# One hybrid decoder layer on one core: the gate weights' low parts on VectorE, and some work put behind the second norm's second root

## The chip, the cores and the metric

The kernel runs on one core of a Trainium2 chip. It uses TensorE (PE in the profile), VectorE (DVE), ScalarE (ACT), GpSimd (POOL) and SyncE (SP), which here only issues transfers. The metric is the device time of one execution in microseconds (us); less is better. Every quoted time of the kernel before is from its runs or its one profiled execution.

## The reference

One layer of a hybrid decoder for 1024 prompt positions and 8 x 8 sample positions, width 1024, hidden width 2816, all in float32:

```python
h = rms_norm(x, norm_mix_g)
proj = h @ w_in
...                                   # convolution heads a, attention heads o
x = x + jnp.concatenate([a, o], axis=-1) @ w_out
h = rms_norm(x, norm_ffn_g)           # the second norm
g_full = jnp.concatenate([ffn_past, h @ w_ffn_gate], axis=1)
g = depthwise_conv_valid(g_full, ffn_conv_w, ffn_conv_b)
x = x + (jax.nn.silu(g) * (h @ w_ffn_up)) @ w_ffn_down
```

The change lies between the last part of `@ w_out` and the first products with `w_ffn_gate` and `w_ffn_up`.

## The kernel before

**Numbers.** Each float32 operand of a product is split in a high part (ScalarE rounds it with a copy) and a low part (the operand less its high part, on VectorE or GpSimd); three matmuls stand for one: high by high, low by high, high by low. Tiles have 128 partitions. Activations lie transposed, as 8 tiles `x2` of 128 x 1088 (1024 prompt and 64 sample positions), worked on in two halves of 544 columns (HN).

**Order.** Tiles of a pool are handed out by tag; a tile laid where an older one was waits for the older one's last users. A scheduler then puts every engine's instructions in one order, which the engine follows strictly; `tc.issue_after(y)` keeps an instruction behind y in that order. Line numbers below are those of the kernel before; in the changed kernel they are 1 to 3 higher behind the edits.

**The stretch around the change** (some 557 to 690 us of the profiled execution):

1. `load_input` loads the mixer's last two tiles by halves (`mx`, high `mh` at line 991, low `ml` at 992). The last slices of `w_out` come as `wr`; `parts_of` (lines 976 to 980) makes their high part on ScalarE (978) and low part on GpSimd (979). Last of all it does the same for the four half tiles of the first gate weights (`gate_raw`; parts `wa`, `wb`).
2. `out_half(0)`: for each of 8 tiles m, matmuls (`g`), then VectorE adds them to `x2` (line 1148), ScalarE squares (1153, `sq`), VectorE sums the squares (1157). Then `out_half(1)` for the second half of the columns; its first three tiles have a deferred part of the product besides.
3. **First root**: `root` adds the squares over partitions with ten matmuls by a column of ones (line 209), and VectorE and ScalarE take the reciprocal root (213 to 224; the square root itself is 219). In PE's order these ten stand behind two tiles of `out_half(1)`. The low parts of the first up weights (1179, VectorE) stand behind the root. `spread` lays the root over partitions (transposes, line 236; copy `rb`, 238). VectorE then scales `x2` (1162), and `split` makes high (1051) and low parts (1052) of block b11 (tiles 0 to 3) and b21 (4 to 7).
4. `first_half(gate0)`: products of the first gate pair with b11 into two PSUM tiles `px`, `py`, copies of them (`ta`, 1200), products with b21, copies again (`c1`, 1205). The **second root** lies between these: its ten matmuls in the last step of b21, its transposes behind it.
5. `early_sums(w_gate, 1)` forms two sums of the second gate pair's weights on VectorE (1086 to 1088, tiles `s` and `wr`) and splits them (high 1075 on ScalarE, low 1076 on GpSimd).
6. `first_half(up0)`, and `second_half` for gate and up with blocks b22 and t1. From here on each pair is seven block products instead of eight, out of sums of blocks (Strassen-like), until 1080 us, when the down projection begins.

```python
        def early_sums(w, j):
            ...
            with tc.issue_after(made[7]):              # the low part of b21's last tile
                nc.vector.tensor_add(s1, u1, u2)
```

Of the kernel before, what the change touches and what calls it, by code (L numbers as in the profile page):

```python
# [18 lines left out]
F32 = mybir.dt.float32  # L19
F32R = mybir.dt.float32r  # L20
AF = mybir.ActivationFunctionType
# [3 lines left out]
P = 128  # L25
# [37 lines left out]
ORDER, DEFER = (4, 5, 6, 7, 0, 1, 2, 3), 3  # L63
# [20 lines left out]
def trunk_kernel(tc, xT, w_in, w_out, w_gate, w_up, w_down, par, kc, vc, sa, sf, pmask, smask,  # L84
                 yT, kT, vT, ca, cas, cf):
    nc = tc.nc
    with (
# [8 lines left out]
        def nm(s):  # L96
            cnt[0] += 1
            return f"{s}_{cnt[0]}"
# [23 lines left out]
        def zt(z, tag, bufs, s, w=N, dt=F32):  # L122
            return zone[z].tile([P, w], dt, tag=tag, name=nm(s), bufs=bufs)
# [76 lines left out]
        rooted, summed, copied, squared = [None], [None], [None], [None]  # L200
# [84 lines left out]
        wr = [wp.tile([P, D], F32, tag="WR", name=nm("wr"), bufs=WR) for _ in range(2)]  # L285
        w0 = [[wp.tile([P, D], F32R, tag="W", name=nm(s)) for s in ("wh", "wl")] for _ in range(2)]
        h = []
# [620 lines left out]
        def pair(s="g", tag="g2"):  # L908

            return zone[pairs[0] + "ps"].tile([P, 1024], F32, tag=tag, name=nm(s), bufs=pairs[1])  # L910
# [4 lines left out]
        def slot(tag, s, dt=F32R, w=HN):  # L915
            return zt("F", tag, 8, s, HN, dt)[:, :w]
# [17 lines left out]
        def two_products(outs, ws, x, start, hook=lambda k, last: None):  # L934


            n = HN // 2
            nk = len(x)
            last = None
            for k, (xh, xl) in enumerate(x):  # L940
                with tc.issue_after(last) if last else nullcontext():
                    for o, (whi, wlo) in zip(outs, ws):
                        for c in range(2):
                            ps = o[:, PO:512] if c == 0 else o[:, 512:PO + HN]
                            t = slice(c * n, c * n + n)
                            nc.tensor.matmul(ps, whi[:, k, :], xh[:, t], start=(start and k == 0), stop=False,
                                             skip_group_check=True)
                            nc.tensor.matmul(ps, whi[:, k, :], xl[:, t], start=False, stop=False,
                                             skip_group_check=True)
                            end = nc.tensor.matmul(ps, wlo[:, k, :], xh[:, t], start=False, stop=(k == nk - 1),  # L950
                                                   skip_group_check=True).ins
                last = end
                hook(k, last)

        def all_of(ps):
            return ps[:, PO:PO + HN]
# [15 lines left out]
        n1 = PARTS[-2]  # L972
# [3 lines left out]
        def parts_of(raw, hi, lo):  # L976

            done = nc.scalar.activation(hi, raw, AF.Copy).ins
            nc.gpsimd.tensor_sub(lo, raw, hi.bitcast(F32))
            return done  # L980
# [3 lines left out]
        def load_input(i, h, tag):  # L984
            nonlocal last_load, last_high
            raw = slot("b11", "mx", F32)
            with tc.issue_after(last_load):
                last_load = nc.sync.dma_start(raw, mixed[k0 + i][:, h * HN:h * HN + HN]).ins
            hi, lo = early[tag].pop() if early[tag] else slot(tag, "mh"), slot(tag, "ml")
            with tc.issue_after(last_high):  # L990
                last_high = nc.scalar.activation(hi, raw, AF.Copy).ins
            lows_made.append(nc.vector.tensor_sub(lo, raw, hi.bitcast(F32)).ins)
            part[h].append((hi, lo))
# [4 lines left out]
        def queued(dst, src):  # L998
            nonlocal last_load
            with tc.issue_after(last_load):  # L1000
                last_load = nc.sync.dma_start(dst, src).ins

        last_load, last_high = weights_read[0], turned_out[0]
        wl = [None] * KT
        raw_wd = {m: slot("b22", "wr", F32, n1 * P) for m in ORDER[:DEFER]}
        for h, tag in enumerate(("b11", "t2")):
            load_input(0, h, tag)
            for m0 in ORDER[h * 4:h * 4 + 4:2]:
                raw = slot("t1", "wr", F32, 2 * n * P)
                queued(raw.rearrange("p (m c) -> p m c", m=2), w_out[m0:m0 + 2, :, k0 * P:].rearrange("m p c -> p m c"))  # L1010
                if m0 == ORDER[h * 4]:
                    load_input(1, h, tag)
                hi, lo = early["b21"].pop() if early["b21"] else slot("b21", "wh", w=512), slot("b21", "wl", w=512)
                with tc.issue_after(last_high):
                    last_high = parts_of(raw, hi, lo)
                hi, lo = [t.rearrange("p (k c) -> p k c", c=P) for t in (hi, lo)]
                for j in range(2):
                    wl[m0 + j] = hi[:, j * n:j * n + n], lo[:, j * n:j * n + n]
# [6 lines left out]
        for i in range(n1):  # L1025
            hi, lo = slot("t3", "mh"), slot("t3", "ml")
            raw = lo.bitcast(F32)
            queued(raw, mixed[kd + i][:, HN:])
            with tc.issue_after(last_high):
                last_high = parts_of(raw, hi, lo)  # L1030
            highs.append(last_high)
            deferred.append((hi, lo))
        for m in ORDER[:DEFER]:
            hi, lo = [slot("b22", t, w=n1 * P) for t in ("wh", "wl")]
            with tc.issue_after(last_high):
                last_high = parts_of(raw_wd[m], hi, lo)
# [4 lines left out]
        gate0 = [[t.rearrange("p (k c) -> p k c", c=P) for t in x] for x in tiles]  # L1041
        for r, (hi, lo) in zip(gate_raw, tiles):
            with tc.issue_after(last_high):
                last_high = parts_of(r, hi, lo)

        blocks = {tag: [None] * 4 for tag in BTAGS}
        made, high = [], [None]
# [12 lines left out]
        def weight_raw(w, j):  # L1060
            raw = []
            for i in (j, j + HF):
                raw.append(wp.tile([P, D], F32, tag="WR", name=nm("wr"), bufs=WR))
                with tc.issue_after(last_load):
                    nc.sync.dma_start(raw[-1], w[i])
            return raw

        def block_tile(x, zone=False):

            if zone:  # L1070
                t = zt("F", "WA", 2, "wa", D, F32R)
            else:
                t = wp.tile([P, D], F32R, tag="W", name=nm("wb"))
            hi, lo = t[:, :half], t[:, half:]
            nc.scalar.activation(hi, x, AF.Copy)  # L1075
            nc.gpsimd.tensor_sub(lo, x, hi.bitcast(F32))  # L1076
            return [t.rearrange("p (k c) -> p k c", c=P) for t in (hi, lo)]

        def early_sums(w, j):

            g, u = weight_raw(w, j)
            g1, u1, u2 = g[:, :half], u[:, :half], u[:, half:]
            t = zt("F", "us", 1, "s1", 3 * HN)
            s1, s2 = t[:, :half], t[:, HN:HN + half]
            with tc.issue_after(made[7]):
                nc.vector.tensor_add(s1, u1, u2)
            nc.vector.tensor_sub(u1, g1, u1)
            nc.vector.tensor_sub(s2, s1, g1)
            with tc.issue_after(squared[0]):
                blocks = [block_tile(s2), block_tile(s1)]  # L1090
            return g, u, s2, blocks
# [101 lines left out]
        def first_half(w, between=lambda: None, hook=lambda k, last: None):  # L1193

            a11, a12, a21, a22 = w
            o = pair("px"), pair("py")
            two_products(o, (a11, a21), blocks["b11"], True)
            shared = [early["shared"].pop(0) if early["shared"] else zt("F", "tmp", 4, "ta", HN) for _ in o]
            for t, ps in zip(shared, o):
                nc.scalar.activation(t, all_of(ps), AF.Copy)  # L1200
            between()
            two_products(o, (a12, a22), blocks["b21"], False, hook)
            kept = [slot("t4", "c1", F32) for _ in o]
            for t, ps in zip(kept, o):
                nc.scalar.activation(t, all_of(ps), AF.Copy)
            return kept, shared

        def second_half(w):
# [6 lines left out]
        def between():  # L1215
            rs.append(root(sq1, D, HN))
# [6 lines left out]
        first_blocks(0, "b11")  # L1223
        first_blocks(4, "b21")
        g1, g_shared = first_half(gate0, between, spread_second)
        ready = early_sums(w_gate, 1)
        r1 = rs[1]
        for k in range(4):
            scale(1, k + 4, r1)
            split(x2[k + 4][:, HN:], "b22", k)  # L1230
        u1, u_shared = first_half(up0)
        for k, (x11, x12, x21, x22) in enumerate(quads):
            scale(1, k, r1)
# [386 lines left out]
        for i, (t0, n) in enumerate(TAIL):  # L1620
            r = []
# [111 lines left out]
```

## Time and profile before

| | |
|---|---|
| median of 3 runs | 1343.35 us (1338.85 to 1350.83) |
| profiled execution, its own time | 1340.95 us |
| its span in the profile | 1339.1 us (1.85 us lie around it) |
| busy: PE / DVE / ACT / POOL | 97% / 70% / 42% / 36% |
| granted PE clock, mean | 0.987 of full |

In rows of the timeline the columns are start, duration, engine, line, operation, output and inputs, shape, and how many are joined; brackets tell how long the engine had been idle and who released it. When several are joined, the duration is from the first one's start to the last one's end. In rows by stretch they are the stretch, its length, each engine's busy time with its instructions, the granted clock (1.00 is full), the share of the DMA engines, and GB/s. In rows of waits: the waiting group, who released it, total us, times, longest.

### The profile page before, as it was taken

The numbers are of one execution on the slowest core, as the hardware profiler recorded it, in microseconds if no ns is written. First come the engines' busy times: TensorE is split into PE (matmuls) and PEld (weight loads), VectorE is DVE, ScalarE is ACT, GpSimd is POOL, SyncE is SP. The second block draws the span as 40 slices with busy tenths as digits, with TensorE's granted clock in tenths as the row PEclk, the third lists the DMA queues.
The fourth block names the chain that finished last, engine by engine and source line by source line (L and its number), as shares of the span: only waits on it lengthen the run. The fifth ranks groups of instructions, "written<-read, shape, count | busy, mean of one in ns | idle before, by whom it ended". The sixth has DMA issues, their size and how long they took to land.

```text
span 1339.1 us, 25960 instructions
## 1 busy us (share of the span) xinstructions
PE 1298.5 (97%) x10302; PEld 1255.0 (94%) x10302; DVE 935.6 (70%) x1786; ACT 561.1 (42%) x1129; POOL 484.9 (36%) x393
## 2 busy tenths in 40 slices
PE   8999999999999998999999999999999989999996
PEld 7999998998988887899999999999999989999996
DVE  6379879565675666579986767667776569767656
ACT  6412121546675566345533323333333344334432
POOL 1312112111101101741665646556465434444610
PEclk9999999999999999989999999999999999999998
DMA  8248867565779867641113322133222395352403
GB/s 311 58 127 292 290 231 195 179 175 147 211 238 270 253 225 249 225 184 43 49 74 122 118 95 90 65 122 108 105 75 79 123 336 188 107 182 89 156 33 102
DMA packets 94233, 211.70 MB, mean 158 GB/s; under 512 B 13984, under 2 KB 43296, under 8 KB 94112
## 3 DMA queue, kind: packets, MB, share of 16 engines
q1 hardware_dynamic: 94112, 210.05, 47.7%
q8 instruction: 81, 1.33, 0.4%
q14 instruction: 40, 0.33, 0.1%
HBM read 153.97 MB, written 56.04 MB: 157 GB/s over the span
## 4 chain that ended last, share of the span: by engine, by line
PE 86%; DVE 7%; DMA 4%; ACT 2%; issue 1%; SPq 0%; DVEq 0%; ACTq 0%
PE g L187 6%; PE g L188 6%; PE g L189 6%; PE g L930 5%; PE g L929 5%; PE g L927 5%; PE py L929 4%; PE py L930 4%; PE py L927 4%; PE px L927 3%; PE px L930 3%; PE px L929 3%; PE pz L929 3%; PE pz L927 3%; PE pz L930 3%; PE o L747 3%
## 5 line engine op out<-in xcount | busy, mean ns | idle before, releaser
L163 POOL TENSOR_TENSOR wl<-wr,wh 128x1024 fp32r<-128x1024 f32 (+1 forms) x36 | 67.3, 1871 | 272.3 <-PE g L189 162.9
L187 PE MATMUL g<-xh,wh 128*128 128x384 f32 (+1 forms) x472 | 157.6, 334 | 2.1 <-DVE qkv L450 1.4
L188 PE MATMUL g<-xl,wh 128*128 128x384 f32 (+1 forms) x472 | 156.0, 330 | 0.0
L189 PE MATMUL g<-xh,wl 128*128 128x384 f32 (+1 forms) x472 | 155.8, 330 | 0.0
L929 PE MATMUL g<-ux,as 128*128 128x272 f32 x504 | 145.8, 289 | 3.6 <-DVE ux L1452 3.6
L930 PE MATMUL g<-ux,as 128*128 128x272 f32 x504 | 146.0, 290 | 0.0
L927 PE MATMUL g<-ux,as 128*128 128x272 f32 x504 | 145.6, 289 | 0.1
L1076 POOL TENSOR_TENSOR wb<-wr,wb 128x512 fp32r<-128x512 f32 x79 | 114.2, 1455 | 50.5 <-ACT wb L1075 50.5
L1467 POOL TENSOR_TENSOR as<-ar,as 128x640 fp32r<-128x640 f32 (+1 forms) x56 | 91.3, 1640 | 107.6 <-ACT as L1466 107.6
L1075 ACT ACTIVATE wb<-wr 128x512 fp32r<-128x512 f32 x79 | 49.6, 628 | 155.1 <-DVE wr L1110 95.1
L929 PEld LDWEIGHTS g<-ux,as 128*128 128x128 f32 x504 | 95.3, 189 | 4.3 <-DVE ux L1452 4.3
L1076 POOL TENSOR_TENSOR wa<-wr,wa 128x512 fp32r<-128x512 f32 x40 | 64.9, 1625 | 92.9 <-ACT wa L1075 75.6
L927 PEld LDWEIGHTS g<-ux,as 128*128 128x128 f32 x504 | 95.7, 190 | 0.3 <-ACT ux L1451 0.3
L930 PEld LDWEIGHTS g<-ux,as 128*128 128x128 f32 x504 | 95.5, 190 | 0.0
L187 PEld LDWEIGHTS g<-xh,wh 128*128 128x128 f32 x472 | 89.3, 189 | 4.7 <-issue 2.3
L1335 DVE SCALAR_TENSOR_TENSOR fc<-gb,prm,fc 128x1104 f32<-128x1104 f32 x44 | 81.6, 1875 | 14.8 <-ACT fc L1333 14.4
L699 ACT ACTIVATE y<-y,m 128x128 f32<-128x128 f32 (+1 forms) x192 | 88.5, 464 | 5.4 <-DVE m L687 5.0
L188 PEld LDWEIGHTS g<-xl,wh 128*128 128x128 f32 x472 | 89.4, 189 | 0.1
L189 PEld LDWEIGHTS g<-xh,wl 128*128 128x128 f32 x472 | 89.3, 189 | 0.1
L400 DVE SCALAR_TENSOR_TENSOR cacc<-gp,prm,cacc 128x1024 f32<-128x1024 f32 x60 | 84.6, 1410 | 0.1
L161 ACT ACTIVATE wh<-wr 128x1024 fp32r<-128x1024 f32 (+1 forms) x36 | 29.6, 821 | 130.4 <-PE g L189 92.5
L662 DVE CUSTOM_DVE_ANT_0 y<-s,pmk 128x128 f32<-128x128 f32 (+1 forms) x192 | 63.7, 377 | 27.3 <-PE s L658 22.1
(386 smaller groups left out, 4308.4 us busy)
## 6 DMA issues: line engine op xcount, KB each, us to landing
cr<-in_kc SPq DMA_DIRECT2D x24, 768.0 KB, 8.1
cr<-in_vc SPq DMA_DIRECT2D x24, 768.0 KB, 6.9
ux<-ub SPq DMA_DIRECT2D x63, 272.0 KB, 4.0
kk<-dk SPq DMA_DIRECT2D x48, 256.0 KB, 5.4
wr<-in_w_in SPq DMA_DIRECT2D x20, 512.0 KB, 4.8
wr<-in_w_gate SPq DMA_DIRECT2D x20, 512.0 KB, 3.3
wr<-in_w_up SPq DMA_DIRECT2D x20, 512.0 KB, 3.8
ub<-u SPq DMA_DIRECT2D x18, 544.0 KB, 4.3
```

The costliest lines, as they stand in the source:

```text
L163: lo_eng.tensor_sub(lo, raw, hi.bitcast(F32))
L187: nc.tensor.matmul(ps[c], whi[:, k, :], xh[:, t0:t0 + n], start=(k == 0), stop=False)
L188: nc.tensor.matmul(ps[c], whi[:, k, :], xl[:, t0:t0 + n], start=False, stop=False)
L189: nc.tensor.matmul(ps[c], wlo[:, k, :], xh[:, t0:t0 + n], start=False, stop=(k == nk - 1))
L400: eng.scalar_tensor_tensor(acc[:, :S], gp[:, j:j + S], col(w0 + j), acc[:, :S], op0=ALU.mult, op1=ALU.add)
L699: nc.scalar.activation(y, y, AF.Exp, bias=m[:, 4 * g + i:4 * g + i + 1], scale=-1.0, accum_out=den[:, g, 2 * hd + u, i:i + 1])
L927: nc.tensor.matmul(ps, whi[:, k, :], xh[:, t], start=(start and k == 0), stop=False, skip_group_check=True)
L929: nc.tensor.matmul(ps, whi[:, k, :], xl[:, t], start=False, stop=False, skip_group_check=True)
L930: last = nc.tensor.matmul(ps, wlo[:, k, :], xh[:, t], start=False, stop=(stop and k == nk - 1), skip_group_check=True).ins
L1076: nc.gpsimd.tensor_sub(lo, x, hi.bitcast(F32))
L1335: nc.vector.scalar_tensor_tensor(c[:, :W], gb[i][:, t:t + W], col(C_FW + 3 * f + t), c[:, :W], op0=ALU.mult, op1=ALU.add)
L1467: nc.gpsimd.tensor_sub(lo, raw, hi.bitcast(F32))
```

## The change

Three edits:

1. The low parts of the four gate half tiles are made on VectorE instead of GpSimd; the high parts stay on ScalarE.
2. `early_sums` of the second gate pair stands behind the end of the second root instead of behind b21's last low part; the `c1` copies of `px` and `py` stand behind the second root's square root.
3. Block b11's first tile `mx` is allotted ahead of block b22's three raw slices of `w_out`, so that the two tags change places in memory.

```diff
-        raw_wd = {m: slot("b22", "wr", F32, n1 * P) for m in ORDER[:DEFER]}
         for h, tag in enumerate(("b11", "t2")):
             load_input(0, h, tag)
+            if not h:
+                raw_wd = {m: slot("b22", "wr", F32, n1 * P) for m in ORDER[:DEFER]}
...
         for r, (hi, lo) in zip(gate_raw, tiles):
             with tc.issue_after(last_high):
-                last_high = parts_of(r, hi, lo)
+                last_high = nc.scalar.activation(hi, r, AF.Copy).ins
+            nc.vector.tensor_sub(lo, r, hi.bitcast(F32))
...
-            with tc.issue_after(made[7]):
+            with tc.issue_after(rooted[0]):
                 nc.vector.tensor_add(s1, u1, u2)
...
-            for t, ps in zip(kept, o):
-                nc.scalar.activation(t, all_of(ps), AF.Copy)
+            with tc.issue_after(squared[0]):
+                for t, ps in zip(kept, o):
+                    nc.scalar.activation(t, all_of(ps), AF.Copy)
```

**VectorE, end of `out_half(0)`.** `sq_6752` gathers the sum of squares, `x_1120` is the last tile of the first half, `x_1127` the first of the second half; `wa` and `wb` are the gate weights' parts. Before:

```order
L1148 TENSOR_TENSOR x_1120_6082<-g_6862,x_1120_6082 128x544
L1157 TENSOR_TENSOR sq_6752<-sq_6805,sq_6752 128x544
L1157 TENSOR_TENSOR sq_6752<-sq_6823,sq_6752 128x544
L1157 TENSOR_TENSOR sq_6752<-sq_6841,sq_6752 128x544
L1157 TENSOR_TENSOR sq_6752<-sq_6859,sq_6752 128x544
L1148 TENSOR_TENSOR x_1127_6122<-g_6880,x_1127_6122 128x544
L1157 TENSOR_TENSOR sq_6752<-sq_6877,sq_6752 128x544
L213 TENSOR_SCALAR rv_6940<-g_1295_6934 128x4
```

Now:

```order
L1150 TENSOR_TENSOR x_1120_6082<-g_6862,x_1120_6082 128x544
L1159 TENSOR_TENSOR sq_6752<-sq_6805,sq_6752 128x544
L1159 TENSOR_TENSOR sq_6752<-sq_6823,sq_6752 128x544
L1159 TENSOR_TENSOR sq_6752<-sq_6841,sq_6752 128x544
L1046 TENSOR_TENSOR wa_6611<-wr_6674,wa_6611 128x512
L1046 TENSOR_TENSOR wa_6612<-wr_6675,wa_6612 128x512
L1046 TENSOR_TENSOR wb_6709<-wr_6676,wb_6709 128x512
L1046 TENSOR_TENSOR wb_6710<-wr_6677,wb_6710 128x512
L1159 TENSOR_TENSOR sq_6752<-sq_6859,sq_6752 128x544
L1150 TENSOR_TENSOR x_1127_6122<-g_6880,x_1127_6122 128x544
L1159 TENSOR_TENSOR sq_6752<-sq_6877,sq_6752 128x544
L213 TENSOR_SCALAR rv_6940<-g_1295_6934 128x4
```

The four low parts stand in front of the last two sums, on whose end the first root's ten matmuls wait. GpSimd's queue loses the same four and has no instruction between the last `w_out` low part and the second gate pair's.

**ScalarE, second root**, from the high part of b21's last tile; `c_1339` and `c_1340` are the `c1` copies, `wb` the second gate pair's high parts, `rb` the spread root. Before:

```order
L1051 ACTIVATE b21h_7147<-x_1148_6242 128x544
L1205 ACTIVATE c_1339_7278<-px_7151 128x544
L219 ACTIVATE rr_7213<-rr_7213 128x5
L1075 ACTIVATE wb_7290<-s_1343_7286 128x512
L1205 ACTIVATE c_1340_7279<-py_7152 128x544
L1075 ACTIVATE wb_7293<-s_1343_7286 128x512
L1075 ACTIVATE wb_7773<-wr_7284 128x512
L238 ACTIVATE rb_7244<-g_1337_7245 128x512
L238 ACTIVATE rb_7244<-g_1338_7251 128x32
```

Now:

```order
L1053 ACTIVATE b21h_7147<-x_1148_6242 128x544
L219 ACTIVATE rr_7213<-rr_7213 128x5
L1208 ACTIVATE c_1339_7278<-px_7151 128x544
L1208 ACTIVATE c_1340_7279<-py_7152 128x544
L238 ACTIVATE rb_7244<-g_1337_7245 128x512
L238 ACTIVATE rb_7244<-g_1338_7251 128x32
L1077 ACTIVATE wb_7290<-s_1343_7286 128x512
L1077 ACTIVATE wb_7293<-s_1343_7286 128x512
L1077 ACTIVATE wb_7773<-wr_7284 128x512
```

The square root stands ahead of both copies, and the spread root's copy ahead of the three weight parts.

**VectorE, second root**, from the low part of b21's last tile to the root's last step (224). Before:

```order
L1052 TENSOR_TENSOR b21l_7148<-x_1148_6242,b21h_7147 128x544
L1086 TENSOR_TENSOR s_1343_7286<-wr_7284 128x512
L1087 TENSOR_TENSOR wr_7284<-wr_7282,wr_7284 128x512
L1088 TENSOR_TENSOR s_1343_7286<-s_1343_7286,wr_7282 128x512
L213 TENSOR_SCALAR rv_7209<-g_1332_7203 128x4
L216 TENSOR_SCALAR rv_7209<-g_1332_7203 32x1
L218 RECIPROCAL rr_7213<-rv_7209 128x5
L222 TENSOR_TENSOR rt_7216<-rr_7213 128x5
L223 SCALAR_TENSOR_TENSOR rt_7216<-rt_7216,rv_7209 128x5
L224 SCALAR_TENSOR_TENSOR rr_7213<-rt_7216,rr_7213 128x5
```

Now:

```order
L1054 TENSOR_TENSOR b21l_7148<-x_1148_6242,b21h_7147 128x544
L213 TENSOR_SCALAR rv_7209<-g_1332_7203 128x4
L216 TENSOR_SCALAR rv_7209<-g_1332_7203 32x1
L218 RECIPROCAL rr_7213<-rv_7209 128x5
L222 TENSOR_TENSOR rt_7216<-rr_7213 128x5
L223 SCALAR_TENSOR_TENSOR rt_7216<-rt_7216,rv_7209 128x5
L224 SCALAR_TENSOR_TENSOR rr_7213<-rt_7216,rr_7213 128x5
L1088 TENSOR_TENSOR s_1343_7286<-wr_7284 128x512
L211 MEMSET rv_14906 128x2
L1089 TENSOR_TENSOR wr_7284<-wr_7282,wr_7284 128x512
L1090 TENSOR_TENSOR s_1343_7286<-s_1343_7286,wr_7282 128x512
```

The three sums went from ahead of the root to behind it.

Through edit 3 a wait changes its place in SP's queue: a matmul of the attention's last product (line 747) was waited for by the second `mx` load and is now waited for by the third raw slice of `w_out`, eight loads later. The scheduler also changed the order in the first pairs behind the norm: on ScalarE the second pair's copy `ta` of its up product stands behind five weight parts and a convolution step, and on PE the first four matmuls of that up product `pz` (blocks t3) stand ahead of 24 matmuls of `px` (block b21) instead of behind them. On SP one `w_up` load and one store of `u` changed places. Each engine has as many instructions as before but for the four that went from GpSimd to VectorE.

## The prediction

> **What bounds the kernel now.** I read the chain of work that ended last first, then busy time by stretches around the change, then what PE waited for there, then the timeline of each engine at those waits.
>
> ```profile
> PE 86%; DVE 7%; DMA 4%; ACT 2%; issue 1%; SPq 0%; DVEq 0%; ACTq 0%
> ```
> ```profile
> 600.00:610.00 10.00, 10.00 (x83) 10.00 (x82) 10.00 (x17) 6.32 (x11) 0.00 (x0) 1.00 0.43 162
> 610.00:620.00 10.00, 9.91 (x79) 9.57 (x78) 9.84 (x18) 3.63 (x7) 0.00 (x0) 1.00 0.02 9
> ...
> 630.00:640.00 10.00, 10.00 (x82) 10.00 (x81) 10.00 (x17) 5.74 (x10) 0.00 (x0) 1.00 0.00 0
> ```
> ```profile
> PE g L209 <- DVE sq L1157: 1.6, 1, 1.6
> PE g L236 <- DVE rv L211: 0.9, 1, 0.9
> ```
>
> PE carries 86% of the chain, so time can be won only where PE waits or runs at a lower clock. Between 600 and 640 us PE and VectorE are both nearly full: PE bounds, and VectorE feeds it without slack. Of PE's waits in the stretch two are touched: 1.6 us at the first root's matmuls (line 209), 0.9 us at the second root's transposes (236). The page gives line 211 as the releaser of the second; the instruction behind which the transposes stand is the root's last step, 224, right ahead of it.
>
> **First root: edit 1.** Here are VectorE, GpSimd, ScalarE and PE at the first wait.
>
> ```profile
> 583.52 7.01 DVE L1157 TENSOR_TENSOR sq<-sq,sq 128x544 f32<-128x544 f32 x4
> 590.46 0.71 DVE L1148 TENSOR_TENSOR x<-g,x 128x544 f32<-128x544 f32 x1
> 591.09 0.71 DVE L1157 TENSOR_TENSOR sq<-sq,sq 128x544 f32<-128x544 f32 x1
> ...
> 594.28 0.17 DVE L224 SCALAR_TENSOR_TENSOR rr<-rt,rr 128x5 f32<-128x5 f32 x1
> ...
> 596.25 1.29 DVE L1179 TENSOR_TENSOR wb<-wr,wb 128x512 fp32r<-128x512 f32 x2
> ...
> 599.92 1.48 DVE L1162 SCALAR_TENSOR_TENSOR x<-x,prm,rb 128x544 f32<-128x544 f32 x2
> ```
> ```profile
> 582.46 1.02 POOL L979 TENSOR_TENSOR wl<-wr,wh 128x384 fp32r<-128x384 f32 x1 [0.37 <-POOL wl L979]
> 583.45 3.02 POOL L979 TENSOR_TENSOR wa<-wr,wa 128x512 fp32r<-128x512 f32 x2
> 586.43 3.52 POOL L979 TENSOR_TENSOR wb<-wr,wb 128x512 fp32r<-128x512 f32 x2
> ```
> ```profile
> 585.35 0.66 ACT L1153 ACTIVATE sq<-x 128x544 f32<-128x544 f32 x1 [0.94 <-DVE sq L1157]
> 587.08 0.66 ACT L1153 ACTIVATE sq<-x 128x544 f32<-128x544 f32 x1 [1.07 <-DVE sq L1157]
> ```
> ```profile
> 590.06 0.29 PE L930 MATMUL g<-mh,wl 128*128 128x272 f32 x1
> 591.95 1.18 PE L209 MATMUL g<-ones,sq 128*128 128x1 f32 x10 [1.60 <-DVE sq L1157]
> 593.05 0.39 PE L927 MATMUL g<-mh,wh 128*128 128x272 f32 x1
> ...
> 598.45 0.77 PE L236 MATMUL g<-ident,rr 128*128 128x128 f32 x5
> ```
>
> Four sums of squares take 7.01 us together, 1.75 us each, exactly while GpSimd makes the gate weights' low parts (583.45 to 589.95). The same sum alone, at 591.09, takes 0.71. So a low part on GpSimd costs VectorE about 1 us beside it. The next add starts 0.63 us behind another's start, and two low parts on VectorE take 1.29 us, so I count 0.64 us for each full-size VectorE instruction in a row with GpSimd idle.
>
> With the order of the changed kernel: the sums start at 583.52, GpSimd having ended its last other low part at 583.48. Three sums end at 585.44, four low parts at 588.0, the fourth sum at 588.6, the add at 589.3, the last sum at 589.95. Their high parts and squares are there: ScalarE's two late squares waited for sums that free a buffer, and these come at 584.2 and 584.8 instead of 585.3 and 587.0. The matmul before the ten starts at 590.06, and matmuls of 272 columns follow each other by 0.125 (83 in 10 us say 0.12), so PE is free for the ten at about 590.2, just behind the sum. They start 1.75 us earlier than 591.95. Bounds: nothing (the low parts take the time that they free) to 1.75; below nothing see the last rival. I take 1.75, the row nearest to the new state being the sum at 591.09 without GpSimd.
>
> The wait has a second price, in the granted clock:
>
> ```profile
> 590.66:594.07 3.41, 2.12 (x18) 2.12 (x19) 1.71 (x6) 1.09 (x3) 0.00 (x0) 0.99 0.23 87
> 594.07:597.49 3.42, 3.42 (x18) 3.42 (x17) 3.38 (x8) 2.40 (x5) 0.00 (x0) 0.51 0.21 81
> ...
> 617.97:621.38 3.41, 2.62 (x22) 2.36 (x20) 2.37 (x10) 1.39 (x4) 0.07 (x1) 1.00 0.00 0
> 621.38:624.79 3.41, 3.33 (x25) 3.15 (x26) 1.41 (x2) 2.32 (x6) 3.41 (x3) 1.00 0.00 0
> ```
>
> Right behind a stretch of 3.41 us in which PE was busy 2.12 us, the clock stood at half for 3.42 us (594.07 to 597.49): half of that, 1.71 us of PE's work, is lost. Behind the second root, where PE was busy 2.62 of 3.41, it stayed full. Without the wait the first stretch would be nearly full, so I take 1.71; bounds 0 and 1.71. The Trainium skill (page "TensorE: Matmul & The Clock Gate", section "What's actually happening") speaks against this term: it has the array fall to half only after at least one idle window of about 3.4 us. By that rule a gap of 1.6 us would not be the cause, and the half clock would stay: the sum would be less by this term. The row at 590.66 does not agree, since PE worked in it.
>
> For PE the two make 3.46 us: the transposes would come at 595.0. VectorE gains less. Its root ends at 594.45 - 1.75 = 592.7; behind it stand four low parts of the up weights, two adds and a sum, seven times 0.64, so that it starts scaling at 597.2, 2.7 us earlier than 599.92. From there it is full up to 617 and PE needs its low parts as they come. **First root: 2.7 us**, with bounds 0 and 3.46.
>
> **Second root: edit 2.**
>
> ```profile
> 617.53 0.69 DVE L1086 TENSOR_TENSOR s<-wr 128x512 f32<-128x512 f32 x1
> ...
> 619.47 0.15 DVE L213 TENSOR_SCALAR rv<-g 128x4 f32<-128x4 f32 x1
> ...
> 620.75 0.17 DVE L222 TENSOR_TENSOR rt<-rr 128x5 f32<-128x5 f32 x1 [0.84 <-ACT rr L219]
> ...
> 621.14 0.17 DVE L224 SCALAR_TENSOR_TENSOR rr<-rt,rr 128x5 f32<-128x5 f32 x1
> ...
> 623.38 6.93 DVE L1162 SCALAR_TENSOR_TENSOR x<-x,prm,rb 128x544 f32<-128x544 f32 x8 [2.07 <-ACT rb L238]
> ```
> ```profile
> 619.99 0.62 ACT L1205 ACTIVATE c<-px 128x544 f32<-128x544 f32 x1 [4.22 <-PE px L950]
> 620.51 0.20 ACT L219 ACTIVATE rr<-rr 128x5 f32<-128x5 f32 x1
> ...
> 622.67 0.68 ACT L238 ACTIVATE rb<-g 128x512 f32<-128x512 f32 x2
> ```
> ```profile
> 618.03 1.10 PE L209 MATMUL g<-ones,sq 128*128 128x1 f32 x10
> ...
> 621.46 0.79 PE L236 MATMUL g<-ident,rr 128*128 128x128 f32 x5 [0.87 <-DVE rv L211]
> ```
>
> VectorE's three weight sums hold the root's first step up to 619.47, though the ten matmuls end about 619.1, and the square root waits on ScalarE behind the copy of `px` (619.99). At the first root, from the end of the ten (593.05, where the next matmul starts) to the root's last end (594.45) there are 1.40 us. Counted from 619.06 this gives 620.46, against 621.31 now: 0.85 us sooner. PE is ready for the transposes at 621.46 - 0.87 = 620.59, and the last step reached it 0.15 us behind its end, so its wait all but goes. **0.85 us**, bounds 0 and 0.87.
>
> What is put behind the root is hidden. The three sums run from 620.46 to 622.4 on the old clock, while VectorE had waited 2.07 us for the spread root, whose copy now follows the transposes at once instead of behind three weight parts. The `c1` copies end before the transposes do, so the next `px` finds its bank free. The three weight parts on ScalarE and their low parts on GpSimd are used in the second gate pair, from 660 us on. If that cover failed, each copy of `px` or `py` would cost PE its 0.62 us.
>
> **The rest.** Edit 3 I cost at nothing, bounds 0.4 us either way.
>
> ```profile
> 546.32 0.27 PE L747 MATMUL o<-ph,vf 128*64 128x128 f32 x1
> ```
> ```profile
> 558.11 0.37 SPq L988 DMA_DIRECT2D mx<-mixed  x1
> ```
>
> The wait that moves in SP's queue is for a matmul that had ended by 546.6, and the load behind it went out at 558.11: it was over in both places, for the `mx` load and for the loads of `w_out`, gate, mixed and up behind the raw slice. In `up`'s first half the copy `ta` of `px` stands ahead of a high part of b22 and that of `py` behind it, each by some 0.55 us: nothing, with 0.4 either way. In the second pair, PE asks four `pz` products 3 us earlier (24 matmuls by 0.125):
>
> ```profile
> 688.83 0.29 PE L927 MATMUL pz<-t3h,wb 128*128 128x272 f32 x1
> ```
> ```profile
> 680.73 2.55 POOL L1076 TENSOR_TENSOR wb<-wr,wb 128x512 fp32r<-128x512 f32 x2
> ```
>
> Their weight part is the first of the two, ready at about 682.0; they would be asked at 685.8. That leaves 3.8 us, and both move with PE: nothing.
>
> **Sum:** 2.7 + 0.85 = 3.55 us, from the profiled execution's 1340.95 to 1337.4. That execution lies 2.4 us under the median of the three runs (1343.35); from the median the same sum gives 1339.8. I take the middle, 1338.6.
>
> **Rivals.**
>
> *The half clock stays.* For it: the clock is granted by stretches whose place no row ties to the program. Against it: the two pairs of rows above. Then PE has 1.75 and 0.85 of gain: 1338.35 from the profiled time, 1339.55 on the middle. The skill's rule named above would give this.
>
> *The low parts only take the place of the slow sums.* For it: VectorE gets 4 x 0.64 = 2.6 us of new work in front of the sum that PE waits for. Against it: the slow sums lose 4 x 1.1 = 4.4. Then only the second root gains: 1340.1, or 1341.3.
>
> *The gain is lost later.* At 1080 us the down projection begins behind loads, and it could begin no sooner. Against it: its loads and weight parts wait for the last products, so they move with PE. Then the time stays: 1340.95, or 1342.1.
>
> *Slower.* The place is the same end of `out_half(0)`. If the low parts ran at 1.75 us each, like the sums now, the last sum would end at 583.52 + 4 x 1.75 + 6 x 0.64 = 594.4, 2.6 us later than 591.8; less the second root's 0.85 the kernel is 1.75 slower, 1342.7 or 1343.9. It decides from about 1.1 us a low part on. For it: ScalarE writes while they run. Against it: GpSimd, beside which the sums were slow, is idle by then.
>
> **Chances.** Forecast 0.58; half clock stays 0.12; low parts take the place 0.12; lost later 0.10; slower 0.08. For the range: the largest gain, 3.46 + 0.87 + 0.8 = 5.1, from the middle of 1342.15 gives 1337.0, the slower rival 1343.9. The three runs lay 4.5 below and 7.5 above their median; with most of that on each side the range is 1332 to 1347. All cases lie within 1% (13.4 us), about what a measurement of this kernel can tell from no change, so: faster 0.03, same 0.94, slower 0.03.
>
> **What would show it.** Right: no sum of squares over 0.8 us behind 584; four low parts of 0.7 at 585.4; no wait of PE at line 209 of the first root, no half clock behind it; scaling from about 597; no wait over 0.2 at the second root's transposes, which come some 3.5 us earlier than 621.46, and the same distance still at 1080. Wrong: sums or low parts of 1 us and more with GpSimd idle, the half clock in place, or a new wait of PE between 640 and 700.

## Result and profile after

The changed kernel takes 1330.4 us (median of 11 runs, 1326.03 to 1335.53); the kernel before, run beside it, 1338.52 (11 runs, 1332.13 to 1350.83). The ratio is 0.9933, with a 95% interval of 0.9913 to 0.9953: 9.0 us less, 6.3 to 11.6. The forecast was 1338.6 us, 1332 to 1347, and a gain of 3.55; the result lies below that range. Two errors add up: the middle from which I counted, 1342.15, lies 3.6 above what the kernel before takes in more runs, and the gain is over twice as large. The profiled execution took 1331.32 us, with a span of 1329.5 against 1339.1.

The chain that ended last, changed kernel, shares by engine:

```profile
PE 81%; DVE 11%; DMA 5%; issue 1%; ACT 1%; SPq 0%; DVEq 0%; ACTq 0%
```

Whole-run shares don't tell where the time went. I cut the span at five events that both traces have, and compare the lengths (worked out from the starts in the timelines; us). `u` is the tile that becomes the input of the down projection:

| stage | before | after | difference |
|---|---|---|---|
| up to the first square of the norm | 573.42 | 572.60 | -0.82 |
| A: to the first scaling of `x` (first root) | 26.50 | 23.74 | -2.76 |
| B: to the second root's transposes | 21.54 | 20.65 | -0.89 |
| C: to the last sum `u` from `py` (end of the gate and up pairs) | 455.84 | 457.26 | +1.42 |
| D: to the third sum `x` of the down projection | 20.53 | 14.30 | -6.23 |
| E: to the end | 241.27 | 240.95 | -0.32 |

**A and B came as worked out.** VectorE and PE of the changed kernel:

```profile
582.73 2.38 DVE L1159 TENSOR_TENSOR sq<-sq,sq 128x544 f32<-128x544 f32 x3
...
585.02 1.29 DVE L1046 TENSOR_TENSOR wa<-wr,wa 128x512 fp32r<-128x512 f32 x2
...
596.34 1.47 DVE L1164 SCALAR_TENSOR_TENSOR x<-x,prm,rb 128x544 f32<-128x544 f32 x2
```
```profile
589.56 1.18 PE L209 MATMUL g<-ones,sq 128*128 128x1 f32 x10
...
594.52 0.77 PE L236 MATMUL g<-ident,rr 128*128 128x128 f32 x5
...
616.99 0.79 PE L236 MATMUL g<-ident,rr 128*128 128x128 f32 x5
```

A sum of squares takes 0.79 us instead of 1.75, a low part on VectorE 0.65; neither root's matmuls carry a wait any more, and no half clock follows the first root.

**C lost again.** PE's waits of the changed kernel that the kernel before does not have, and ScalarE at the first of them, before (660.85 to 662.45) and after (657.10 to 660.45), and PE at both:

```profile
PE px L927 <- ACT ta L1262: 0.5, 1, 0.5
PE py L927 <- DVE gb L1319: 0.4, 1, 0.4
```
```profile
660.85 1.13 ACT L1337 ACTIVATE fc<-fc 128x1104 f32<-128x1104 f32 x1
661.93 0.63 ACT L1259 ACTIVATE ta<-px 128x544 f32<-128x544 f32 x1
662.45 1.12 ACT L1337 ACTIVATE fc<-fc 128x1104 f32<-128x1104 f32 x1
```
```profile
657.10 1.12 ACT L1340 ACTIVATE fc<-fc 128x1104 f32<-128x1104 f32 x1 [0.79 <-DVE fc L1338]
659.42 1.13 ACT L1340 ACTIVATE fc<-fc 128x1104 f32<-128x1104 f32 x1 [1.19 <-DVE fc L1338]
660.45 0.60 ACT L1262 ACTIVATE ta<-px 128x544 f32<-128x544 f32 x1
```
```profile
661.11 0.39 PE L927 MATMUL px<-b21h,wa 128*128 128x272 f32 x1 [0.51 <-ACT ta L1262]
661.34 0.29 PE L929 MATMUL px<-b21l,wa 128*128 128x272 f32 x1
...
666.96 0.39 PE L927 MATMUL py<-t1h,wb 128*128 128x272 f32 x1 [0.45 <-DVE gb L1319]
667.19 0.29 PE L929 MATMUL py<-t1l,wb 128*128 128x272 f32 x1
```

These are in the gate product of the second pair. The copy `ta` that frees PE's bank stood between the two Silu (the gate's activation function, `fc<-fc`) before; now it stands behind the second, which waits 1.19 us for VectorE.

The two waits are the whole loss. Matmuls otherwise start 0.125 us apart, but the idle time in brackets counts from the end of the matmul ahead, 0.29 us after its start, and the matmul behind a wait is followed only after 0.23. The matmul ahead of the first wait started at 660.31: from there to 661.34 two steps took 1.03 us instead of 0.25, so 0.78 are lost for an idle time of 0.51. From 666.22 to 667.19 it is 0.72 for 0.45. Together that is 1.50, against C's +1.42.

**D is where the unexpected gain lies**: the start of the down projection. Its weights come as raw `ar`; ScalarE makes the high part `as`, GpSimd the low part; of its moving side ScalarE makes the high part `ux`, VectorE the low part. The kernel before, timelines of ScalarE, GpSimd, VectorE and PE, and its windows:

```profile
1077.17 2.62 ACT L1466 ACTIVATE as<-ar 128x640 fp32r<-128x640 f32 x4 [9.60 <-PE py L929]
1079.70 2.83 ACT L1451 ACTIVATE ux<-ux 128x544 fp32r<-128x544 f32 x5
...
1077.99 7.06 POOL L1467 TENSOR_TENSOR as<-ar,as 128x640 fp32r<-128x640 f32 x4 [15.43 <-ACT as L1466]
...
1080.37 6.53 DVE L1452 TENSOR_TENSOR ux<-ux 128x544 fp32r<-128x544 f32 x5 [0.73 <-ACT ux L1451]
...
1083.70 0.39 PE L929 MATMUL g<-ux,as 128*128 128x272 f32 x1 [1.35 <-DVE ux L1452]
...
1085.68 0.60 PE L929 MATMUL g<-ux,as 128*128 128x272 f32 x1 [1.34 <-DVE ux L1452]
```
```profile
1080.00:1085.00 5.00, 1.96 (x10) 1.10 (x8) 4.63 (x3) 4.26 (x8) 5.00 (x3) 1.00 1.04 406
1085.00:1090.00 5.00, 4.32 (x23) 4.32 (x23) 4.96 (x9) 0.24 (x1) 0.05 (x1) 0.66 0.58 201
```

The changed kernel, the same four engines:

```profile
1064.42 2.60 ACT L1469 ACTIVATE as<-ar 128x640 fp32r<-128x640 f32 x4
...
1065.21 6.14 POOL L1470 TENSOR_TENSOR as<-ar,as 128x640 fp32r<-128x640 f32 x4 [5.71 <-ACT as L1469]
...
1075.15 3.26 DVE L1455 TENSOR_TENSOR ux<-ux 128x544 fp32r<-128x544 f32 x5
...
1077.08 0.30 PE L927 MATMUL g<-ux,as 128*128 128x272 f32 x1
```

Before, ScalarE stood 9.60 us at an `as` high part until PE had done its last product with b22; GpSimd's low parts then ran beside VectorE's, which took 1.31 us each on average (one by one 1.29, 2.06 and 2.06 beside GpSimd, then 0.71 twice), and PE waited for `ux` three times (3.6 us in all in the waits) and got a lower clock (0.66 in the second window). Now ScalarE begins 12.8 us earlier, 9.7 of them beyond the 3.05 by which all work around is earlier; GpSimd ends at 1071.35 before VectorE begins, VectorE's low parts take 0.65 each, and PE does not wait. The memory explains the earlier start: the four `as` tiles lie at bytes 156,864 to 177,344 of each partition; b22 filled 160,640 to 178,048 there before, and with edit 3 b11 does, whose last product ends 15 us earlier (1059 against 1074 in the changed kernel).

### The profile page after: what moved, and what is told of

Read it like the earlier page. It is cut to its first block, busy times and chain, and to the rows that moved or that the text cites. A ratio compares the mean times of both kernels' runs of the same rounds, so it can differ in the third digit from the quotient of the medians.

```text
span 1329.5 us, 25961 instructions
## 1 busy us (share of the span) xinstructions
PE 1290.9 (97%) x10302; PEld 1249.3 (94%) x10302; DVE 928.3 (70%) x1790; ACT 561.9 (42%) x1129; POOL 479.3 (36%) x389
## 4 chain that ended last, share of the span: by engine, by line
PE 81%; DVE 11%; DMA 5%; issue 1%; ACT 1%; SPq 0%; DVEq 0%; ACTq 0%
PE g L187 6%; PE g L189 6%; PE g L188 6%; PE g L930 5%; PE g L929 5%; PE g L927 5%; PE py L929 4%; PE py L927 4%; PE py L930 4%; PE pz L929 3%; PE pz L927 3%; PE pz L930 3%; PE px L927 3%; PE px L930 3%; PE px L929 3%; PE s L658 3%
## 5 line engine op out<-in xcount | busy, mean ns | idle before, releaser
L929 PE MATMUL g<-ux,as 128*128 128x272 f32 x504 | 144.8, 287 | 0.0
L929 PEld LDWEIGHTS g<-ux,as 128*128 128x128 f32 x504 | 94.7, 188 | 0.0
L662 DVE CUSTOM_DVE_ANT_0 y<-s,pmk 128x128 f32<-128x128 f32 (+1 forms) x192 | 63.6, 376 | 30.1 <-PE s L658 26.8
```

## Experiments

Each kernel was profiled once and, but for one, timed beside the kernel before; ratios are to that, and the brackets behind a name hold the edits in it. The stage differences, worked out as above, are sharper than the times: C of six kernels agrees with before within 0.04 us where edit 2 is absent. The stretch ahead of A is left out of the table. It differs from before by -6.0 (e4) to +5.7 us (e8) without following the edits (e10, which touches only tiles of the down projection, has -4.2), so much of the scatter of the times lies there; the mean granted clock in it is 1.00 in e4 and 0.98 in e8.

| kernel | ratio (95% interval) | A | B | C | D | E |
|---|---|---|---|---|---|---|
| changed kernel | 0.9933 (0.9913-0.9953) | -2.76 | -0.89 | +1.42 | -6.23 | -0.32 |
| e1_layout (3) | 0.9939 (0.9910-0.9967) | -0.41 | -0.02 | 0.00 | -6.24 | -0.34 |
| e2_no_layout (1, 2) | 0.9982 (0.9959-1.0005) | -2.76 | -0.88 | +1.44 | +1.04 | +0.58 |
| e3_low_parts (1) | 0.9988 (0.9969-1.0006) | -3.73 | -0.02 | +0.04 | +0.46 | -0.14 |
| e4_second_root (2) | 0.9985 (0.9965-1.0006) | +0.08 | -0.88 | +1.38 | -0.17 | +0.01 |
| e5_no_second (1, 3) | 0.9934 (0.9911-0.9956) | -3.72 | 0.00 | +0.03 | -6.23 | -0.28 |
| e6_sums_only | one run | -3.72 | -0.89 | +1.42 | -6.24 | -0.56 |
| e7_copies_only | 0.9933 (0.9918-0.9948) | -3.73 | -0.56 | +1.12 | -6.23 | +0.91 |
| e8_as_on_t4 | 1.0006 (0.9989-1.0023) | -2.71 | -0.89 | +1.42 | +4.31 | +0.41 |
| e9_ux_first | 1.0000 (0.9979-1.0021) | -1.60 | -0.02 | +0.02 | -0.08 | +0.89 |
| e10_as_past_rc | 0.9926 (0.9898-0.9954) | -0.11 | -0.02 | 0.00 | -6.23 | -0.22 |
| e11_as_low_dve | 0.9995 (0.9977-1.0013) | +0.27 | -0.01 | 0.00 | -5.64 | +2.89 |
| e12_beside | 0.9980 (0.9959-1.0001) | -3.72 | -0.88 | +1.46 | -0.77 | +0.29 |

**The three edits apart.** The hunks of the diff above, applied singly or in pairs.

*e1_layout*, edit 3 alone: 

> Only edit 3, on the kernel before. Theory A (memory): the down projection's first `as` tiles lie on b22 in the kernel before and on b11 with edit 3; the wait of ScalarE for the last products with b22 (9.6 us up to 1077.2) goes, and with it PE's waits for `ux` (3.6 us) and the half clock behind them (3.4 us, 1.7 of PE's work). Then the kernel gains 5.3 to 6.2 us, about 1332.5 against 1338.5, while both norm waits (1.6 and 0.9) stay as they are. Theory B (arrival): the start of the down projection improved because the work came there 3 us earlier, by edits 1 and 2; then this kernel takes the time of the kernel before, 1338 to 1339, and the 3.6 us of waits for `ux` stay.

*e2_no_layout*, edits 1 and 2: 

> Edits 1 and 2 without edit 3. Theory A: both norm waits go, scaling starts about 2.9 us earlier, the second root's transposes about 3.8 us earlier, some 3.0 us are left at 1060, and the waits for `ux` at the start of the down projection (3.6 us) with the half clock stay: 1335 to 1336, a gain of 3.0. Theory B: the waits for `ux` are gone here too: about 1330, the whole gain of 8 to 9 us.

Waits of e1_layout, then of e2_no_layout:

```profile
PE g L209 <- DVE sq L1158: 1.6, 1, 1.6
PE g L236 <- DVE rv L211: 0.9, 1, 0.9
```
```profile
PE g L929 <- DVE ux L1454: 3.6, 3, 1.3
```

With edit 3 alone both norm waits stay, no `ux` wait is left and D shrinks by 6.24; without it the 3.6 us stay to the tenth and D does not shrink. Theory A (memory) holds, theory B (arrival) falls: counted from the first square, e2 comes 3.6 us earlier to the second root and 2.2 us earlier to D, and gains nothing at D (1.04 longer; the half clock there lasts 6.8 us instead of 3.4). The intervals of e2 and of the changed kernel do not touch.

*e3_low_parts*, edit 1 alone: 

> Edit 1 alone. By the prediction's steps: no sum of squares over 0.8 us, no wait of PE at the first root's ten matmuls, no half clock behind them, scaling 2.7 to 2.9 us earlier, the second root's wait of 0.9 still there; of that 2.0 to 2.7 us at the end, 1336 to 1336.5, with the waits for `ux` as before. If the half clock behind the first root came from its own period and not from the gap, PE gains only 1.2 to 1.75 us. Theory B would allow more than 2.9 us at the end, since the work comes to the down projection earlier.

The time cannot be told from no change; the stage can. A is 3.73 shorter, and 3.71 us are still there at 1080, so nothing of edit 1 is lost on the way. A has a scatter of its own: a half-clock stretch just ahead of the first square (569.4 to 572.8 in the changed kernel) is missing in this execution, and then PE arrives sooner and 0.5 us of the wait is left. With that stretch, A is 26.1 to 26.8 in the four kernels without edit 1 (26.50 before) and 23.7 to 23.8 in the three with it; without the stretch it is 24.90 (e9_ux_first) and 26.39 (e10_as_past_rc, where the half clock behind the root lasts 6.8 us) against 22.8 in the five with edit 1. Edit 1 is worth 2.1 to 3.6 us.

*e4_second_root*, edit 2 alone: 

> Edit 2 alone. The first root with its wait of 1.6 us and its half clock stays; the second root's wait (0.9) shrinks to under 0.2, and PE gains 0.85 us there; 1337.5 to 1338 at the end, hardly to be told from no change. The new short waits of PE between 640 and 670 us in the changed kernel (0.5 for the copy `ta`, 0.4 for the sum `gb`) should be absent or smaller here if they come from PE's earlier arrival, and as large if they come from the moved sums and copies.

B gains 0.88 as worked out, C loses 1.38: edit 2 alone costs half a microsecond. The waits for `ta` (0.5) and `gb` (0.4) are here in full although PE arrives only 0.8 us earlier, and e3, where it arrives 3.7 us earlier, has neither. So they belong to edit 2, not to the earlier arrival.

**Which half of edit 2.** *e5_no_second*, without it:

> Edits 1 and 3 without edit 2. From the runs so far edit 2 wins 0.8 us at the second root and loses 1.4 us again between 640 and 690, where ScalarE's copy `ta` of the first `px` stands behind the second Silu. If these 1.4 us belong to edit 2, then here: the 0.9 us at the second root's transposes stay, no wait for `ta` and none for `gb` in that stretch, a shift of 2.8 us against the kernel before kept from the scaling to 1077, and 6.2 to 6.6 more at the start of the down projection: 9.2 us in all against before, 0.5 less than or the same as the changed kernel, 1329.5 to 1331. If they come from PE's earlier arrival, the waits of 0.5 and 0.4 are here too and the gain is 8 us.

*e6_sums_only*, the changed kernel with the `c1` copies back in place:

> The changed kernel with the `c1` copies where they were before: of edit 2 only the three sums stand behind the second root. If the moved sums are what puts ScalarE's `ta` copy behind the second Silu, the waits of 0.5 and 0.4 between 655 and 665 are here; the second root's transposes wait up to 0.3 us, since the copy of `px` may hold the square root by its 0.6 us. If the copies are what costs, both waits are gone.

*e7_copies_only*, the changed kernel with the sums back behind `made[7]`:

> The changed kernel with the three sums where they were before: of edit 2 only the `c1` copies stand behind the square root. If the sums cause the later waits, there is no wait for `ta` and `gb` here, and the shift at the scaling (2.8 us) is kept to 1077; the second root still waits for the sums on VectorE, 0.5 to 0.9 us. Then 1329 to 1330.5, 0.5 to 1.4 us less than the changed kernel. If the copies cause them, the waits of 0.5 and 0.4 stay and nothing is won at the root: 1331.5.

e5 did as expected: no `ta` and no `gb` wait, C unchanged. The moved sums (e6) win 0.89 and lose 1.42, with both waits: they change the order on ScalarE. For e7 I had expected the loss to go; it did not. The `ta` and `gb` waits are gone, but the moved copies bring another one, seen on PE and, behind three high parts, on ScalarE:

```profile
623.15 0.39 PE L946 MATMUL px<-b21h,wa 128*128 128x272 f32 x1 [1.26 <-ACT ta L1202]
...
620.48 2.11 ACT L1053 ACTIVATE b22h<-x 128x544 fp32r<-128x544 f32 x3 [1.02 <-DVE x L1164]
622.49 0.61 ACT L1202 ACTIVATE ta<-px 128x544 f32<-128x544 f32 x1
```

B gains 0.56 and C loses 1.12. Either half of edit 2 gives back more than it wins; leaving it out (e5, 1329.77 us) cannot be told from the changed kernel by the time.

**Where the `as` tiles lie.** *e8_as_on_t4*, the changed kernel with

```diff
+        zt("D", "AS", 4, "as", 2 * n0 * P, F32R)
         for tag in OUT[::-1]:
             zt("D", tag, RING, "uh", N)
-        zt("D", "AS", 4, "as", 2 * n0 * P, F32R)
```

> The changed kernel with the four `as` tiles of the down projection laid ahead of the `ux` tiles in its zone, so that they lie on the last-used block t4 instead of b11; the front is that of the changed kernel. Theory A (the tiles' place in memory decides): ScalarE's high parts wait for the last products with t4, at about 1079.5, that is for PE's very last work in the stage; PE then waits for the first high and low part, at least 0.65 + 1.5 us, and for the `ux` parts queued behind on ScalarE: 3 to 6 us of waits and 1.7 us of half clock, so 1335 to 1338 against 1330.4 of the changed kernel. Theory B' (edit 3 works through the order of the first loads): no wait at 1080, 1330 to 1331.

*e10_as_past_rc*, the kernel before with

```diff
+        zt("D", "RC", RAWS["RC"], "ar", n0 * P)
         zt("D", "AS", 4, "as", 2 * n0 * P, F32R)
-        for tag in ("RC", "RB", "RA"):
+        for tag in ("RB", "RA"):
```

> The kernel before, none of the three edits, with the down projection's `as` tiles laid behind the raw tiles RC instead of ahead of them: they then lie on b11 and on t1, which is used last by the products 5 us ahead of those with b22, and RC lies on b22 in their place. By the memory theory ScalarE's high parts start at about 1072 and the waits for `ux` shrink to under 0.5 us or go, so 4 to 6 us less, unless RC's loads (for the third product, needed from some 1110) come late, which PE would show as a wait for `as` at 1110 to 1130. If edit 3 worked by anything at the front (the order of the loads of `mx` and the `w_out` slices), the time stays 1339.

e8, ScalarE, GpSimd, VectorE and PE, and one window:

```profile
1083.81 2.61 ACT L1469 ACTIVATE as<-ar 128x640 fp32r<-128x640 f32 x4 [12.77 <-PE pz L930]
1086.33 4.47 ACT L1454 ACTIVATE ux<-ux 128x544 fp32r<-128x544 f32 x8
...
1084.62 7.03 POOL L1470 TENSOR_TENSOR as<-ar,as 128x640 fp32r<-128x640 f32 x4 [18.59 <-ACT as L1469]
...
1087.00 6.50 DVE L1455 TENSOR_TENSOR ux<-ux 128x544 fp32r<-128x544 f32 x5 [5.24 <-ACT ux L1454]
...
1087.02 0.39 PE L927 MATMUL g<-ux,as 128*128 128x272 f32 x1 [3.25 <-ACT ux L1454]
```
```profile
1090.00:1095.00 5.00, 3.76 (x15) 3.45 (x16) 5.00 (x7) 0.80 (x2) 1.65 (x1) 0.50 0.00 0
```

The later the block under `as` is used, the later ScalarE starts: counted from the last sum `u` from `py`, 9.8 us ahead of it on b11, 0.1 ahead on b22, 3.0 behind it on t4. D is 4.31 longer than before and 10.5 longer than in the changed kernel: I had expected 3 to 6 us of waits (6.0 came) and 1.7 of half clock, and the half clock lasted 10.2 us; the time, 1341.55 us, lies above my 1335 to 1338. e10 gains the whole of D, 6.23, and no other stage of the table moves by over 0.3, with none of the edits and with edit 3's tags unmoved. So the front, which edit 3 also touches, has no part in it:

```profile
1067.56 2.00 ACT L1467 ACTIVATE as<-ar 128x640 fp32r<-128x640 f32 x3 [3.74 <-PE py L929]
...
1068.38 4.65 POOL L1468 TENSOR_TENSOR as<-ar,as 128x640 fp32r<-128x640 f32 x3 [2.91 <-ACT as L1467]
...
1073.86 3.26 DVE L1453 TENSOR_TENSOR ux<-ux 128x544 fp32r<-128x544 f32 x5
```

**What the late start costs.** ScalarE's queue, or GpSimd beside VectorE? *e9_ux_first*, the kernel before with `ux_high` a list of the `ux` high parts and

```diff
-            nc.scalar.activation(hi, raw, AF.Copy)
+            with tc.issue_after(ux_high[4]) if not done else nullcontext():
+                nc.scalar.activation(hi, raw, AF.Copy)
```

> The kernel before (its memory, none of the three edits), with one order changed: ScalarE's four first high parts `as` stand behind the fifth high part `ux` instead of ahead of the first. The `as` tiles still lie on b22. If the price at the start of the down projection is that the `ux` parts queue behind `as` on ScalarE and are then made beside GpSimd, it goes here too: `ux` high parts from about 1071, low parts of 0.65 each done before 1080, `as` high parts still at 1077.2 and their low parts (1.77 each) just ahead of the 3.75 us that PE takes for each tile: no wait for `ux`, no half clock, 5 to 6 us less, 1333 to 1334 against 1339. If the late place of `as` is a price by itself, PE now waits for `as` instead, for 2 us or more, and the half clock stays.

```profile
1071.98 1.36 ACT L1451 ACTIVATE ux<-ux 128x544 fp32r<-128x544 f32 x2 [0.80 <-DMA ux<-ub]
1074.17 2.62 ACT L1467 ACTIVATE as<-ar 128x640 fp32r<-128x640 f32 x4 [0.82 <-PE py L929]
...
1074.98 7.05 POOL L1468 TENSOR_TENSOR as<-ar,as 128x640 fp32r<-128x640 f32 x4 [15.45 <-ACT as L1467]
...
1076.56 7.33 DVE L1452 TENSOR_TENSOR ux<-ux 128x544 fp32r<-128x544 f32 x5
```

My theory of the queue fell. The high parts were early, but VectorE still came to its low parts while GpSimd was at work, and they took 1.47 us each on average; PE waited 4.0 us for `ux`. I had not seen that VectorE works on `u` until 1075 in any case.

*e11_as_low_dve*: e9 with the first four low parts on VectorE.

```diff
-            nc.gpsimd.tensor_sub(lo, raw, hi.bitcast(F32))
+            if done:
+                nc.gpsimd.tensor_sub(lo, raw, hi.bitcast(F32))
+            else:
+                first_low = nc.vector.tensor_sub(lo, raw, hi.bitcast(F32)).ins
+                for l in lows[1:5] if m == 0 else late[-4:] if m == 3 else ():
+                    behind(l, first_low)
```

> As the kernel with `ux` first (memory of the kernel before, none of the three edits, `as` high parts behind five `ux`), and besides the first four `as` low parts are made on VectorE instead of GpSimd: the first behind the first `ux` low part, the other three behind the fifth, ahead of `u`'s last products. `as` still lies on b22 and its high parts still wait for b22's last product. Theory G (GpSimd beside VectorE is the price: four `as` low parts for 7.05 us there make five `ux` low parts take 7.33 us instead of 3.26): with GpSimd idle each `ux` low part takes 0.65 again, each `as` low part about 0.8, PE waits for `ux` under 0.5 us, no half clock, and the kernel gains 5 to 6 us against before, 1333 to 1334. Theory P (the late place in memory is a price by itself): VectorE has 3.2 us more work between 1075 and 1084, PE waits for `as` or `ux` 3 us or more as before, no gain.

```profile
1075.52 2.63 DVE L1452 TENSOR_TENSOR ux<-ux 128x544 fp32r<-128x544 f32 x4
1078.06 2.29 DVE L1471 TENSOR_TENSOR as<-ar,as 128x640 fp32r<-128x640 f32 x3
...
1113.52 0.39 PE L930 MATMUL g<-ux,as 128*128 128x272 f32 x1 [2.62 <-POOL as L1469]
```

With GpSimd idle the `ux` parts take 0.65 again though `as` still lies on b22; PE does not wait at the start and keeps its clock, and D shrinks by 5.64. The first 120 matmuls of the projection end 15.6 us after the last `pz`, against 21.3 before and 15.0 in the changed kernel. Half of the gain goes in E, at 1113, where PE waits 2.62 us for another `as`, whose low part took GpSimd 3.21 us beside VectorE; D and E together gain 2.75, which the time (1337.36 us, where I had expected 1333 to 1334) does not show. As a repair it fails; on the cause it speaks for GpSimd.

*e12_beside*, the changed kernel, with GpSimd's first `as` low parts made to wait for VectorE's first `ux` low part:

```diff
-            nc.gpsimd.tensor_sub(lo, raw, hi.bitcast(F32))
+            low = nc.gpsimd.tensor_sub(lo, raw, hi.bitcast(F32)).ins
+            if not done:
+                tc.add_manual_dep(low, lows[0].name, mybir.DependencyInfo(mybir.DependencyClass.Sync, ...))
```

> The changed kernel, its memory and its high parts untouched (`as` on b11, high parts at about 1064.4 to 1067); only the four first `as` low parts on GpSimd wait until VectorE has made its first `ux` low part (about 1075.9), so that they run beside the other four. Theory G (GpSimd beside VectorE is the price at the start of the down projection): the `ux` low parts take about 1.3 each instead of 0.65, PE waits for them 2 to 4 us in three or four pieces, with or without the half clock, and the kernel is 2 to 5.5 us slower than the changed one: 1332.5 to 1336. Theory P (the place in memory, or that ScalarE's queue stands, is the price): nothing of that, since both are as in the changed kernel; 1330 to 1331, with at most one wait of 0.5 for the first `as` low part.

```profile
1070.28 7.95 POOL L1470 TENSOR_TENSOR as<-ar,as 128x640 fp32r<-128x640 f32 x4 [16.45 <-DVE ux L1455]
...
1069.48 7.34 DVE L1455 TENSOR_TENSOR ux<-ux 128x544 fp32r<-128x544 f32 x5
...
1074.88 0.39 PE L929 MATMUL g<-ux,as 128*128 128x272 f32 x1 [1.31 <-DVE ux L1455]
...
1076.88 0.39 PE L929 MATMUL g<-ux,as 128*128 128x272 f32 x1 [1.36 <-DVE ux L1455]
```

The memory is that of the changed kernel and the high parts are early (the fifth `ux` high part ends at 1068), yet 5.46 of D's 6.23 us are back (the two waits for `ux` and the half clock behind them, and one of 0.47 us for the first `as`), 1335.94 us against 1330.4; the two intervals do not touch. GpSimd beside VectorE is the price, and the memory swap paid because it took the one out of the other's way.

## Why the prediction was wrong

- **The step that failed: "Edit 3 I cost at nothing, bounds 0.4 us either way."** It measured -6.23. I followed the tags only to the loads at 558 us, where the swap is made, not to the tiles that lie there 500 us later. The row `as<-ar ... [9.60 <-PE py L929]` stood in the trace of before, and so did PE's 3.6 us of waits for `ux`.
- **The rival "the gain is lost later" held the same error**: "its loads and weight parts wait for the last products, so they move with PE" takes that wait as given. Which product they wait for is set by the memory under them, and edit 3 changed that.
- **First root: right.** Predicted 2.7 with bounds 0 and 3.46; measured 2.76 at the scaling, 3.11 at the transposes (predicted 3.46). In the five kernels with edit 1 and full clock just ahead of the first square, 0.5 us of the wait stays, which the sum did not have. The half clock behind the root is there in all six kernels without edit 1 and in none of the eight with it, so the rival that it stays falls. The rule of the Trainium skill (page "TensorE: Matmul & The Clock Gate", section "What's actually happening"), by which only an idle window of about 3.4 us lowers the clock, does not agree with these runs: a wait of 1.4 to 1.6 us was enough. The length of the wait alone does not decide it, though: behind the 2.62 us at 1113 in e11_as_low_dve the clock stayed full.
- **Low parts that only take the sums' place, and the slower rival: no.** The low parts took 0.65 us each, the sums 0.79.
- **Second root: the gain was right (0.85; measured 0.89), its cover was not.** "What is put behind the root is hidden" failed: the moved sums cost +1.42, by the two waits in the second pair's gate product, for which the sum has no term (a new wait between 640 and 700 is only named as a sign of being wrong). I had checked data that arrive in time, not what else the moved sums reorder on ScalarE. The two "nothing", for `up`'s first half and for the second pair's `pz`, held: no new wait is there.
- **Sum.** -2.76 - 0.89 + 1.42 = -2.23 for edits 1 and 2, against -3.55; edit 3 added -6.23, which no case of mine had.
- **D in pieces.** Counted by starts, as in C, the three waits of 3.6 us idle cost PE 4.4 us, a short one ahead of the projection's first matmul (1080.39) 0.3, and the half clock 1.5 (for 3.4 us matmuls start 0.23 us apart instead of 0.125): 6.2, the whole of D.

## What to carry to other kernels

A change of memory layout is priced at every later stage that lies on the moved bytes: find the tiles that come there, what they wait for, and who runs beside whom once that wait moves. An instruction on GpSimd is not free because GpSimd has time: look at what VectorE does in the same microseconds. And a group of instructions that is "put behind" something can change the order of other engines too (here three VectorE sums changed ScalarE's); read the new order at the places where PE's banks are freed.

## What the hardware showed that I had not expected

Five `ux` low parts alone take 3.26 us and four `as` low parts alone 6.14; run beside each other in e12 they take 7.34 and 7.95, as if taking turns: one by one, the last three `ux` parts take 2.07 to 2.08 us instead of 0.72 and the `as` parts 1.97 to 2.04 instead of 1.57, each kind starting 2.0 us apart. PE's waits for `ux` come 2.0 us apart too. It is not always VectorE that pays: in e11 an `as` part that began at 1082.53, with VectorE already at work, took 4.84 us, while the four `ux` parts beside it took 0.72 to 0.73. By what rule the one or the other pays, these runs do not show. Sums that read PSUM are not touched: in the kernel before, a sum `gb` takes 0.65 with GpSimd idle and another 0.66 beside it.

```profile
675.10 0.65 DVE L1318 TENSOR_TENSOR gb<-pz,tb 128x480 f32<-128x480 f32 x1
...
680.00 0.66 DVE L1318 TENSOR_TENSOR gb<-py,ta 128x480 f32<-128x480 f32 x1 [1.93 <-PE py L930]
```
```profile
679.49 1.29 POOL L1076 TENSOR_TENSOR wb<-s,wb 128x512 fp32r<-128x512 f32 x1
```

The Trainium skill says so (page "GPSIMD Engine Reference", section "8. Key points"): GpSimd shares its SBUF interfaces with VectorE and disturbs VectorE's instructions that have two SBUF inputs. This trace agrees, for `sq` and `ux` (two SBUF inputs, slowed) and for `gb` (one input in PSUM, not slowed).
